# The low halves of the streamed weights: from GpSimd to VectorE in a two-layer hybrid encoder

## The chip, the core and the metric

The kernel runs on one core of a Trainium2 chip. The core has five engines that work side by side and meet at semaphores: TensorE (PE; its weight loads are listed as PEld), VectorE (DVE), ScalarE (ACT), GpSimd (POOL) and SyncE (SP), which here only issues transfers (DMA). Each engine works through its own queue in order: an instruction that waits holds up all that stand behind it. The metric is the time of one execution in device microseconds; several runs are told by their median.

## The reference

A trunk of two encoder layers over 1040 positions (16 learned ones ahead of 1024) with 1024 channels. Each layer has a mixer and a feed-forward part:

```
for l in range(DEPTH):
    h = h + hybrid_mixer(rmsnorm(h, norm1_w[l]), w_in[l], ...)
    h = h + swiglu(rmsnorm(h, norm2_w[l]), w_gate_up[l], w_down[l])
h = rmsnorm(h, final_norm_w)

def hybrid_mixer(h, w_in, conv_qkv_w, a_log, dt_bias, dn_norm_w, sc_conv_w, w_out):
    proj = h @ w_in
    qkv, z, b_raw, a_raw, sc_b, sc_c, sc_h = jnp.split(proj, idx, axis=-1)
    ...                      # q, k, v: short convolution, silu; q and k normalised
    o_fwd = chunk_gated_delta_rule(qp, kp, vp, gp[:, :, 0], bp[:, :, 0])
    o_bwd = flip(chunk_gated_delta_rule(flip(qp), flip(kp), flip(vp), ...))
    ...                      # o: sum of both, normalised, times silu(z)
    y_sc = sc_b * depthwise_conv_centred(sc_c * sc_h, sc_conv_w)
    return jnp.concatenate([o, y_sc], axis=-1) @ w_out

def swiglu(h, w_gate_up, w_down):
    gate, up = jnp.split(h @ w_gate_up, 2, axis=-1)
    return (jax.nn.silu(gate) * up) @ w_down
```

All of it is float32.

## The kernel before

**Products in two parts.** Channels lie on the 128 partitions, positions along the free axis. Each operand of a large product is split into a high part (the value rounded to a narrower float32 format that TensorE multiplies, `F32R`) and a low part (the rest). A product is then three matmuls: high weight by high x (line 157), high weight by low x (158), low weight by high x (159), all summed in one PSUM bank. `dense` (line 146) does this for a tile of 128 output channels, in two or three chunks of positions, and after each chunk takes the sum out of its bank (`evac`), on VectorE.

**How a weight tile is made.** `wload` (133) takes a tile in pieces of at most four 128x128 blocks, that is 128x512 elements. For each piece `wsplit` (124) issues the transfer of the raw weights on SP's queue (129), the high part on ScalarE (130) and the low part as raw minus high (131). Line 131 stands on VectorE where the flag `lov[0]` is set and on GpSimd elsewhere. Raw pieces have two buffers, high and low parts three each, so a high part waits until TensorE has left an earlier piece's buffer.

**Where line 131 runs.** `wload` and `wsplit` serve three products:

- the in-projection (`inproj`, 290), 28 tiles of two pieces in a layer. In the loop over `seq` (k heads, then q heads) the flag is set from the fifth tile on (line 632: `lov[0] = pos > 3`) and stays so through the v tiles; the loop behind them, with the gates z and the convolution group, sets it for its first two steps alone (line 738: `lov[0] = j < 2`). So of the 56 pieces of a layer 18 are on VectorE.
- the out-projection: eight pieces for the convolution half (918) and, in `out_part` (941), eight for each of two halves of the positions. The flag is not set.
- "the rest of down": four of the 22 blocks of the hidden axis, which the down projection takes as a plain product, eight pieces of four blocks. In layer 0 they are loaded between its chunks (1423, 1449), in layer 1 in one go by `last_weights` (1392). The flag is not set.

The gate-up projection and the larger part of down go by a seven-product scheme (Strassen's) with sums and differences of weight blocks and of x blocks; its weights are split by `w_op` (993, lines 997 and 998) and `w_unit`, whose low parts are on VectorE already.

**What else is on the two engines.** VectorE evacuates the banks (line 296 and 720 in the in-projection, 905 in the out-projection and rest of down), makes the low parts of x (178), does the short convolutions (309, 310), the triangular inversion (523, 525), the scan's state and outputs (795, 836, 858, 865, 868), and, in the second half of the out-projection, the scaled sums of x blocks for the seven-product scheme (`t_sum`, 977; `t_split`, 965) and the running sum of squares for the norm (950). GpSimd has, besides line 131, a few products with rstd (716, 732), with each other (729), a subtraction in `finalize` (857), most of the low parts of O (929) and some transfers (412, 415, 608 to 612).

**Order.** The program gives each instruction a priority (by its place in the text, or set by hand: `at_prio`, `mmp`, `evp`), and a planner (line 1573) simulates the engines and lays down each engine's queue from the priorities and from when it thinks that an instruction is ready. The delta-rule scan has high priority; the products of the in-projection fill TensorE between its steps. The out-projection follows: all eight tiles of the first half of the positions (`out_part(0, m)`), then all eight of the second (`out_part(1, m)`), with the sums of x blocks made beside the second.

Of the kernel before, what the change touches and what calls it, by code (L numbers as in the profile page):

```python
# [7 lines left out]
F32 = mybir.dt.float32  # L8
# [3 lines left out]
ALU = mybir.AluOpType  # L12
# [30 lines left out]
def trunk(ctx: ExitStack, tc: tile.TileContext, xT, w_in, w_ba, w_out, w_gu, w_dn,  # L43
# [8 lines left out]
    def nm(p):  # L52
        cnt[0] += 1
        return f"{p}_{cnt[0]}"
# [45 lines left out]
    tt = nc.vector.tensor_tensor  # L100
    stt = nc.vector.scalar_tensor_tensor
    ts = nc.vector.tensor_scalar
    ptt = nc.gpsimd.tensor_tensor
# [18 lines left out]
    lov = [False]  # L122

    def wsplit(src, hi, lo, raw=None):

        kk = src.shape[1]
        if raw is None:
            raw = wp.tile([128, WK, 128], F32, tag="raw", bufs=2, name=nm("raw"))
        dma(raw[:, 0:kk, :], src)
        whi_done[0] = act(out=hi, in_=raw[:, 0:kk, :], func=AF.Copy)  # L130
        (tt if lov[0] else ptt)(out=lo, in0=raw[:, 0:kk, :], in1=hi.bitcast(F32), op=ALU.subtract)  # L131

    def wload(src, nk):

        res = []
        step = min(nk, WK)
        for k0 in range(0, nk, step):
            kk = min(step, nk - k0)
            hi = wp.tile([128, WK, 128], F32R, tag="whi", name=nm("whi"))
            lo = wp.tile([128, WK, 128], F32R, tag="wlo", name=nm("wlo"))  # L140
            wsplit(src[:, k0:k0 + kk, :], hi[:, 0:kk, :], lo[:, 0:kk, :])
            for k in range(kk):
                res.append((hi[:, k, :], lo[:, k, :]))
        return res
# [135 lines left out]
    for l in range(DEPTH):  # L280
# [1111 lines left out]
        def last_weights(m):  # L1392
            if not fin_w:
                fin_w.append(flat(Y[0][2], F32R)[:, 0:4096].rearrange("p (m k e) -> p m k e", m=8, k=4))
                rows = [row(Y[1], F32R, 3) for _ in range(3)] + [row(Y[1] + "f", F32R)]
                fin_w.append([r[:, 512 * q:512 * q + 512].rearrange("p (k e) -> p k e", k=4) for r in rows for q in range(2)])
            hi, lo = fin_w[0][:, m], fin_w[1][m]
            wsplit(w_dn[l, m, :, 0:NF, :], hi, lo, raw4(("raw", "ck2")[m % 2]))
            wds.append([(hi[:, k], lo[:, k]) for k in range(4)])
# [11 lines left out]
        for u, (p, b, m) in enumerate(UNITS):  # L1411
# [16 lines left out]
            for j in range(NJ):  # L1428
# [9 lines left out]
                if b == NBK - 1:  # L1438
                    dh, z, op = TO[p]
# [138 lines left out]
```

## Time and profile before

| | |
|---|---|
| median of three runs | 2513.88 us |
| lowest, highest | 2511.24, 2517.37 us |
| the profiled execution, its own time | 2517.22 us |
| its span, first to last instruction | 2515.4 us |
| TensorE's granted clock, mean | 0.997 |
| matmuls | 17508 |
| transfers | 335.27 MB, mean 133 GB/s |

The profiler's page gives, for one execution, the busy time of each engine and its share of the span. A group of instructions is one line of the program on one engine: count, busy time, mean duration in ns, then the idle time of that engine just before them and what ended it. "Idle before <-ACT whi" means that the engine stood idle until ScalarE had finished the high part. In a list of instructions in order of time each row has its start, its duration, the engine, the line and the tiles (written <- read); in brackets stands the idle time before it. A table of windows gives the busy time of each engine within each stretch of the span. Matmuls overlap: the time from one start to the next is shorter than the duration shown, so counts of matmuls in equal windows say more of TensorE's pace than its busy share.

### The profile page before, as it was taken

The numbers are of one execution on the slowest core, as the hardware profiler recorded it, in microseconds if no ns is written. First come the engines' busy times: TensorE is split into PE (matmuls) and PEld (weight loads), VectorE is DVE, ScalarE is ACT, GpSimd is POOL, SyncE is SP. The second block draws the span as 40 slices with busy tenths as digits, with TensorE's granted clock in tenths as the row PEclk, the third lists the DMA queues.
The fourth block names the chain that finished last, engine by engine and source line by source line (L and its number), as shares of the span: only waits on it lengthen the run. The fifth ranks groups of instructions, "written<-read, shape, count | busy, mean of one in ns | idle before, by whom it ended". The sixth has DMA issues, their size and how long they took to land. (4 is left out here: it accounts for less than half of the span.)

```text
span 2515.4 us, 44862 instructions
## 1 busy us (share of the span) xinstructions
PE 2478.2 (99%) x17508; PEld 2276.9 (91%) x17508; DVE 1696.9 (67%) x3073; ACT 1045.9 (42%) x1944; POOL 340.0 (14%) x359
## 2 busy tenths in 40 slices
PE   8999999999999999999999999999999999999998
PEld 6989999999999999999999888998977888887887
DVE  4788333649877777877657893336698777677765
ACT  5554333535333333344445543335453333234444
POOL 1031212331000000000111212133400000000012
PEclk9999999999999999999999999999999999999999
DMA  3444353624323332764224443446332233238541
GB/s 127 135 166 149 112 161 130 212 77 136 116 102 102 108 102 81 256 198 133 92 77 145 152 154 116 143 131 205 120 126 101 97 105 117 90 112 279 177 120 68
DMA packets 199530, 335.27 MB, mean 133 GB/s; under 512 B 23404, under 2 KB 85668, under 8 KB 199316
## 3 DMA queue, kind: packets, MB, share of 16 engines
q1 hardware_dynamic: 171204, 293.84, 35.3%
q10 hardware_dynamic: 25936, 34.19, 4.2%
q0 software_dynamic: 2176, 4.36, 0.6%
q8 instruction: 138, 2.26, 0.4%
q14 instruction: 76, 0.62, 0.1%
HBM read 250.31 MB, written 81.99 MB: 132 GB/s over the span
## 5 line engine op out<-in xcount | busy, mean ns | idle before, releaser
L131 POOL TENSOR_TENSOR wlo<-raw,whi 128x512 fp32r<-128x512 f32 x132 | 176.4, 1338 | 1285.4 <-ACT whi L130 1116.7
L157 PE MATMUL pacc<-a,whi 128*128 128x346 f32 (+1 forms) x808 | 263.6, 329 | 8.8 <-ACT whi L130 7.6
L159 PE MATMUL pacc<-a,wlo 128*128 128x346 f32 (+1 forms) x808 | 262.4, 326 | 0.7 <-DVE wlo L131 0.5
L157 PE MATMUL pacc<-b,whi 128*128 128x346 f32 (+2 forms) x672 | 234.0, 349 | 2.4 <-ACT b L900 1.8
L159 PE MATMUL pacc<-b,wlo 128*128 128x346 f32 (+2 forms) x672 | 233.1, 348 | 0.8 <-DVE wlo L131 0.8
L158 PE MATMUL pacc<-a,whi 128*128 128x346 f32 (+1 forms) x688 | 225.1, 327 | 0.0
L130 ACT ACTIVATE whi<-raw 128x512 fp32r<-128x512 f32 x168 | 106.0, 631 | 228.3 <-PE pacc L158 124.9
L158 PE MATMUL pacc<-b,whi 128*128 128x346 f32 (+2 forms) x580 | 200.8, 346 | 0.0
L157 PEld LDWEIGHTS pacc<-a,whi 128*128 128x128 f32 x808 | 152.2, 189 | 14.6 <-ACT whi L130 8.1
L159 PEld LDWEIGHTS pacc<-a,wlo 128*128 128x128 f32 x808 | 152.9, 189 | 1.7 <-DVE wlo L131 0.8
L157 PEld LDWEIGHTS pacc<-b,whi 128*128 128x128 f32 x672 | 126.9, 189 | 14.5 <-issue 3.1
L159 PEld LDWEIGHTS pacc<-b,wlo 128*128 128x128 f32 x672 | 126.6, 189 | 9.8 <-DVE wlo L131 1.1
L158 PEld LDWEIGHTS pacc<-a,whi 128*128 128x128 f32 x688 | 130.3, 189 | 2.6 <-issue 2.1
L997 ACT ACTIVATE whi<-rw 128x512 fp32r<-128x512 f32 x92 | 57.6, 631 | 140.1 <-PE pf L1016 36.4
L158 PEld LDWEIGHTS pacc<-b,whi 128*128 128x128 f32 x580 | 109.5, 189 | 6.9 <-issue 0.4
L997 ACT ACTIVATE b<-rw 128x512 fp32r<-128x512 f32 x64 | 39.9, 631 | 135.0 <-PE pacc L1016 37.4
L296 DVE TENSOR_TENSOR a<-pacc,rstd 128x346 f32<-128x346 f32 (+2 forms) x59 | 32.7, 555 | 89.6 <-PE pacc L159 89.5
L296 DVE TENSOR_TENSOR b<-pacc,rstd 128x346 f32<-128x346 f32 (+1 forms) x63 | 32.5, 516 | 82.8 <-PE pacc L159 82.8
L131 POOL TENSOR_TENSOR a<-raw,a 128x512 fp32r<-128x512 f32 x3 | 3.9, 1285 | 597.1 <-ACT a L130 597.1
L997 ACT ACTIVATE a<-rw 128x512 fp32r<-128x512 f32 x64 | 40.0, 629 | 101.7 <-PE pacc L1016 60.3
L998 DVE TENSOR_TENSOR wlo<-rw,whi 128x512 fp32r<-128x512 f32 x92 | 62.8, 686 | 4.8 <-ACT whi L997 4.1
L1015 PE MATMUL pacc<-b,whi 128*128 128x260 f32 (+1 forms) x172 | 53.5, 311 | 0.7 <-ACT b L1051 0.7
(966 smaller groups left out, 8012.8 us busy)
## 6 DMA issues: line engine op xcount, KB each, us to landing
raw<-in_w_in SPq DMA_DIRECT2D x112, 256.0 KB, 2.5
raw<-in_w_gu SPq DMA_DIRECT2D x104, 256.0 KB, 2.9
rw<-in_w_gu SPq DMA_DIRECT2D x88, 256.0 KB, 3.0
rw<-in_w_dn SPq DMA_DIRECT2D x94, 192.0 KB, 2.7
rec<-vkd SPq DMA_DIRECT2D x61, 256.0 KB, 2.7
raw<-in_w_out SPq DMA_DIRECT2D x48, 256.0 KB, 2.8
b<-ad SPq DMA_DIRECT2D x45, 260.0 KB, 3.3
a<-ad SPq DMA_DIRECT2D x45, 256.0 KB, 5.2
```

The costliest lines, as they stand in the source:

```text
L130: whi_done[0] = act(out=hi, in_=raw[:, 0:kk, :], func=AF.Copy)
L131: (tt if lov[0] else ptt)(out=lo, in0=raw[:, 0:kk, :], in1=hi.bitcast(F32), op=ALU.subtract)
L157: mm(ps[:, :n], wh, xh[:, n0:n1], start=(k == 0), stop=False)
L158: mm(ps[:, :n], wh, xl[:, n0:n1], start=False, stop=False)
L159: mm(ps[:, :n], wl, xh[:, n0:n1], start=False, stop=(k == K - 1))
L296: tt(out=t[:, n0:n1], in0=ps, in1=rstd[:, n0:n1], op=ALU.mult)
L997: act(out=hi, in_=src, func=AF.Copy)
L998: tt(out=lo, in0=src, in1=hi.bitcast(F32), op=ALU.subtract)
L1015: mm(ps[:, :CW], w[0][:, k, :], th[:, cs], start=first and k == 0, stop=False, skip_group_check=True)
```

## The change

Line 131 no longer looks at the flag: each low part of `wsplit` is made on VectorE. The flag is still set at lines 632 and 738, and nothing reads it. Nothing else differs in the text of the program; the planner lays the queues anew.

```diff
@@ -128,7 +128,7 @@
             raw = wp.tile([128, WK, 128], F32, tag="raw", bufs=2, name=nm("raw"))
         dma(raw[:, 0:kk, :], src)
         whi_done[0] = act(out=hi, in_=raw[:, 0:kk, :], func=AF.Copy)
-        (tt if lov[0] else ptt)(out=lo, in0=raw[:, 0:kk, :], in1=hi.bitcast(F32), op=ALU.subtract)
+        tt(out=lo, in0=raw[:, 0:kk, :], in1=hi.bitcast(F32), op=ALU.subtract)
```

`tt` is VectorE's `tensor_tensor`, `ptt` GpSimd's.

## The prediction

> **What bounds the kernel now.** I read the page first, its busy line and its groups.
>
> ```profile
> span 2515.4 us, 44862 instructions
> PE 2478.2 (99%) x17508; PEld 2276.9 (91%) x17508; DVE 1696.9 (67%) x3073; ACT 1045.9 (42%) x1944; POOL 340.0 (14%) x359
> ```
>
> TensorE is busy for all but 37 us of the span. VectorE has a third of the span free, GpSimd nearly all of it. So work that changes engines counts only where TensorE ends up waiting for it. Next come the groups by line, different shapes apart, for the low parts on GpSimd and on VectorE (count, busy us, mean ns, idle us before them and who ended it), and TensorE's waits (us in total, times, longest).
>
> ```profile
> L131 POOL TENSOR_TENSOR wlo<-raw,whi 128x512 fp32r<-128x512 f32 x132 | 176.4, 1338 | 1285.4 <-ACT whi L130 1116.7 <-PE pacc L158 41.9 <-DMA raw<-in_w_in 38.8
> L131 DVE TENSOR_TENSOR wlo<-raw,whi 128x512 fp32r<-128x512 f32 x36 | 24.7, 686 | 1.9 <-ACT whi L130 1.6
> ```
>
> ```profile
> PE pacc L157 <- ACT whi L130: 8.7, 5, 5.9
> PE pacc L159 <- DVE wlo L131: 1.4, 2, 0.8
> ```
>
> GpSimd needs 1338 ns for a low part, VectorE 686. TensorE never waits for a low part from GpSimd: no such row stands in its waits. It waits twice, 1.4 us, for one of the 36 that VectorE makes already. The halves of a weight tile are made well ahead, so a faster subtraction alone gives nothing.
>
> Where could TensorE feel VectorE? I cut the run at the stages in which GpSimd makes low parts while VectorE is busiest: the two halves of the out-projection in both layers, the rest of down of layer 0, and the last weights (columns: us, then busy us and count of PE, PEld, DVE, ACT, POOL, clock, DMA share, GB/s; below them line 131 alone).
>
> ```profile
> 551.00:578.30 27.30, 27.30 (x231) 27.30 (x230) 18.25 (x36) 16.60 (x27) 11.71 (x10) 1.00 0.60 181
> 578.30:612.40 34.10, 31.88 (x262) 31.43 (x261) 33.99 (x53) 19.41 (x35) 6.20 (x4) 1.00 0.40 129
> 1795.00:1829.60 34.60, 34.60 (x294) 34.60 (x293) 27.99 (x50) 21.34 (x36) 15.31 (x12) 1.00 0.53 177
> 1829.60:1860.00 30.40, 27.60 (x155) 22.66 (x154) 30.36 (x46) 16.86 (x27) 3.57 (x2) 0.94 0.35 113
> 1231.00:1275.00 44.00, 44.00 (x277) 43.73 (x276) 36.44 (x66) 27.45 (x55) 11.97 (x8) 1.00 0.38 138
> 2436.00:2452.00 16.00, 16.00 (x71) 12.87 (x70) 6.00 (x9) 6.94 (x13) 11.70 (x13) 1.00 0.35 96
> ```
>
> ```profile
> 551.00:578.30 27.30, 0.00 (x0) 11.71 (x10) 1.00 0.60 181
> 2436.00:2452.00 16.00, 0.00 (x0) 10.54 (x8) 1.00 0.35 96
> ```
>
> In the second halves VectorE has no free time (33.99 of 34.10, 30.36 of 30.40) and TensorE loses 2.2 and 2.8 us. These two stages, where the next stage's operands are combined, decide most.
>
> **The change, part by part.** *What moves.* 132 subtractions of the first group and the 8 of the last weights (last row above): 140, the same operands, from GpSimd to VectorE. GpSimd loses 187 us (176.4 + 10.5), VectorE gains 140 x 0.686 = 96 us, 1697 to 1793 of 2515. No other instruction is added. The transfers of the raw weights on SP's queue stay; a raw buffer comes free some 0.6 us earlier (1338 - 686 ns), which is worth 0 as long as TensorE waits for no raw transfer, and no such row stands in its waits. On GpSimd's queue, what stood behind a low part (the subtractions and products of lines 716, 732, 857, 929, the transfers of 412 and 608) comes earlier; TensorE stands idle for none of it either. On VectorE's queue the moved instruction can stand before evacuations of matmul banks and before the x, T and scan operands: it waits for ScalarE's high part, and behind it TensorE may wait for a bank or an operand. Where it stands is chosen by the planner, which orders every engine anew.
>
> *Cost in the queue (1).* The 36 on VectorE delayed TensorE by 1.4 us: 0.039 us each, times 140 is 5.4 us. Lower end 0: most of the 140 meet an emptier VectorE than those 36. Upper end: twice it, 10.8, if the waits of the banks behind them add as much. I take 5.4, since it is the only row that shows low parts on this queue.
>
> *The out-projection (2).* In the first halves VectorE is free for 9.1 and 6.6 us and gets 10 and 12 low parts. One costs a full queue 0.60 us, from start to start:
>
> ```profile
> 586.88 0.68 DVE L998 TENSOR_TENSOR wlo<-raw,whi 128x512 fp32r<-128x512 f32 x1
> 587.48 0.42 DVE L905 TENSOR_TENSOR a<-pf,a 128x260 f32<-128x260 f32 x1
> ```
>
> That is 6.0 and 7.2 us: hidden in the first, 0.6 us over in the second, if nothing else gets shorter. Without that cover all 13.2 us would push the full halves. In the full halves there are 4 and 2 low parts: 2.4 and 1.2 us, 3.6 in all, with nothing to hide under. Against that stands what GpSimd does to VectorE there:
>
> ```profile
> 578.60 1.79 DVE L977 SCALAR_TENSOR_TENSOR a<-a,npar 128x520 f32<-128x520 f32 x1
> 583.37 0.68 DVE L950 TENSOR_TENSOR rstd<-rstd,sq 128x520 f32<-128x520 f32 x1
> 586.21 0.74 DVE L977 SCALAR_TENSOR_TENSOR a<-a,npar 128x520 f32<-128x520 f32 x1
> 587.82 1.65 DVE L950 TENSOR_TENSOR rstd<-rstd,sq 128x520 f32<-128x520 f32 x1
> 595.92 1.78 DVE L977 SCALAR_TENSOR_TENSOR a<-a,par,a 128x520 f32<-128x520 f32 x1
> 1832.74 1.66 DVE L950 TENSOR_TENSOR rstd<-rstd,sq 128x512 f32<-128x512 f32 x1
> 1840.69 1.79 DVE L977 SCALAR_TENSOR_TENSOR b<-b,par,b 128x512 f32<-128x512 f32 x1
> ```
>
> ```profile
> 578.54 1.29 POOL L131 TENSOR_TENSOR wlo<-raw,whi 128x512 fp32r<-128x512 f32 x1 [1.39 <-ACT whi L130]
> 587.62 1.30 POOL L131 TENSOR_TENSOR wlo<-raw,whi 128x512 fp32r<-128x512 f32 x1 [4.73 <-DVE wlo L998]
> 595.01 2.13 POOL L131 TENSOR_TENSOR wlo<-raw,whi 128x512 fp32r<-128x512 f32 x1 [6.10 <-PE pf L158]
> 1832.55 1.29 POOL L131 TENSOR_TENSOR wlo<-raw,whi 128x512 fp32r<-128x512 f32 x1 [5.40 <-DVE wlo L998]
> 1839.66 2.28 POOL L131 TENSOR_TENSOR wlo<-raw,whi 128x512 fp32r<-128x512 f32 x1 [5.81 <-ACT whi L130]
> ```
>
> The same line takes 0.74 us (586.21) or 1.79 (578.60), and 0.68 or 1.65. Each long one reads two tensors from SBUF and overlaps a GpSimd subtraction; it ends as that one does. The five cost 1.05, 0.97, 1.04, 0.98 and 1.05 us, 5.1 together, against 3.6 for the same low parts on VectorE. So the ends are -1.5 us (all of the stretch goes and TensorE follows one for one) and +4.2 (3.6 and the 0.6, no relief). I take +0.7, below the middle, because the stretched rows are on the engine that bounds the stage, but its gain is capped by TensorE's waits there.
>
> *Rest of down (3).* VectorE has 7.6 us free of 44.0 and gets 8 x 0.60 = 4.8: hidden, 0. Its cover is thin: TensorE loses nothing there now, and without the cover it would be up to 4.8 us. The last weights: 10.0 of 16.0 us are free, 4.8 needed: 0.
>
> *Clock (4).* Around the end of the scan and in the second full half of layer 1 the clock drops when TensorE has stood still.
>
> ```profile
> 1730.00:1735.00 5.00, 3.20 (x22) 2.65 (x20) 4.03 (x5) 1.92 (x6) 3.79 (x3) 1.00 1.02 381
> 1735.00:1740.00 5.00, 4.75 (x17) 3.88 (x17) 5.00 (x10) 5.00 (x14) 0.00 (x0) 0.66 1.01 407
> 1845.00:1850.00 5.00, 3.56 (x21) 2.78 (x19) 5.00 (x10) 3.21 (x6) 0.00 (x0) 1.00 0.40 131
> 1850.00:1855.00 5.00, 4.12 (x10) 3.00 (x11) 5.00 (x8) 4.27 (x7) 0.00 (x0) 0.66 0.39 131
> 1855.00:1860.00 5.00, 5.00 (x28) 3.49 (x27) 4.96 (x8) 2.08 (x4) 0.00 (x0) 1.00 0.19 63
> ```
>
> The window at clock 0.66 passes 10 matmuls instead of 28: 18/28 of 5 us is 3.2 us lost, 0.9 of it idle, so 2.3 us is the clock. A new wait of this size pays it once more, a removed one gets it back: between -4.6 (both drops go) and +4.6 (two more). I take +0.5, since a fuller queue adds waits more readily than a re-ordered one removes them.
>
> *Sum.* 5.4 + 0.7 + 0 + 0.5 = +6.6 us. The profiled execution took 2517.2 us by its own time, 1.8 us of it outside the span, and becomes 2523.8. The median of the runs shown is 3.3 us lower; against it the forecast is 2513.9 + 6.6 = **2520.5 us**, slower by 0.26%.
>
> **The rivals.** *A, VectorE becomes the bound of the out-projection: slower by more.* A low part on VectorE waits at the head of its queue for ScalarE's high part, which waits for TensorE to leave its buffer: the rows at 595.01 and 1839.66 stood 6.10 and 5.81 us before they could start. If VectorE stands still for a third of that, 2 us, at each of the six low parts in the full halves, that is 12 us, plus two clock drops, 4.6: 2513.9 + 16.6 = 2530. It decides once VectorE's free time there goes below the waits, and there is none. Against it: the planner can put other work first, and the 36 on VectorE idle 1.9 us in all.
>
> *B, the stretch goes and the time falls.* If the full halves lose their 5.1 us of stretch for 3.6 us of work, and the chain that ends the scan (line 1290 at 1.74 us and line 865 at 1.22, elsewhere 0.69 and 0.17, rows below) loses its 2.1, the waits of TensorE there can shrink: 2.2 and 2.8 us in the full halves, 1.8 + 0.3 at 1730 to 1740, and two drops of 2.3. All of it is 11.7; 60%, since not every wait in these windows hangs on a stretched row, is 7: 2507.
>
> ```profile
> 1730.94 1.74 DVE L1290 TENSOR_TENSOR rw<-rw,rw 128x512 f32<-128x512 f32 x1 [3.33 <-POOL a3f L857]
> 1732.60 1.22 DVE L865 SCALAR_TENSOR_TENSOR st<-st,g 128x4 f32<-128x4 f32 x1
> 1741.34 0.17 DVE L865 SCALAR_TENSOR_TENSOR st<-st,g 128x4 f32<-128x4 f32 x1
> 636.74 0.69 DVE L1290 TENSOR_TENSOR rw<-rw,rw 128x512 f32<-128x512 f32 x1 [0.69 <-DMA rw<-in_w_gu]
> ```
>
> The Trainium skill speaks for B: "GPSIMD Engine Reference", section Specifications, says that GpSimd's SBUF interfaces are shared with VectorE, with contention for VectorE instructions that have two SBUF inputs. The trace agrees: 0.74 against 1.79 us for one line. Against B: TensorE waits at few places, and the moved work lands on the same full queue.
>
> *C, hidden either way.* The 96 us fall into VectorE's 818 free ones, the queue cost is near 0, gains and losses of the full halves cancel: 2514, give or take 5.
>
> **How the numbers follow.** Two runs of this kernel can differ by about 0.2%, 5 us; that is my bound of no change. The forecast holds 0.30 (2519 to 2526), A 0.20, B 0.30, C 0.20. Slower is forecast and A, 0.50; faster is B, 0.30; the same is C, 0.20. The likeliest sign is slower, so the time given is the forecast's, whose own range is 2514 (queue cost 0, the rest as summed) to 2528 (5.4 more in the queue and the clock once more). The range for 8 in 10 reaches down into B, to 2504 (10 us of the 11.7), and up through A to 2538 (a second third of the stand-still at two to four of the six).
>
> **What would show it.** Right: rows of TensorE waiting for low parts of line 131 on VectorE, about four times the 1.4 us; the full halves as long as before or longer; VectorE busy somewhat under 1793 us, by as much stretch as goes. Line 977 and line 950 at 0.74 and 0.68 us throughout would show that the stretch was GpSimd's. For A: idle time of VectorE ended by ScalarE's high part between the first and the second half of the out-projection. For B: no clock below 1.00 at the end of the scan and after the out-projection, and fewer than 2 us lost in each full half. Wrong altogether: a time beyond 2538 or under 2504, which would mean that the planner's new order moved the matmuls themselves, far from line 131.

## The result, and the profile after

| | before | changed |
|---|---|---|
| median of 14 runs each | 2516.23 us | 2509.51 us |
| lowest, highest | 2511.24, 2518.01 us | 2506.66, 2514.66 us |
| ratio, 95% interval | | 0.9975 (0.9968 to 0.9982) |
| the profiled execution, its own time | 2517.22 us | 2510.77 us |

The changed kernel is 6.7 us faster by the medians; by the ratio 0.25% (0.18 to 0.32%), 6.3 us. Forecast was 6.6 us slower: the sign was wrong. Rival B had been priced at 7 us faster.

The page of the changed kernel, its span and the busy time of the engines:

```profile
span 2507.8 us, 44856 instructions
PE 2476.0 (99%) x17508; PEld 2277.4 (91%) x17508; DVE 1753.8 (70%) x3213; ACT 1050.2 (42%) x1946; POOL 160.3 (6%) x219
```

VectorE has exactly 140 instructions more (3073 to 3213). At 686 ns they would be 96.0 us, but its busy time, which counts overlapping instructions once, rose by only 56.9. Added up row by row, the durations of all VectorE instructions outside line 131 fell from 1837.77 to 1803.33 us: 34.4 us went out of them, without their number changing. Two lines that the prediction named show it: one line's instructions in min/median/max ns, with the first and last start, first in the kernel before:

```profile
L977 DVE SCALAR_TENSOR_TENSOR a<-a,npar x4: 744/1102/1794, 578.6 to 591.1; 128x520 f32<-128x520 f32 x4
L950 DVE TENSOR_TENSOR rstd<-rstd,sq x28: 676/692/1657, 556.1 to 1855.0; 128x520 f32<-128x520 f32 x14, 128x512 f32<-128x512 f32 x14
```

and in the changed one:

```profile
L977 DVE SCALAR_TENSOR_TENSOR a<-a,npar x4: 750/752/754, 581.5 to 594.8; 128x520 f32<-128x520 f32 x4
L950 DVE TENSOR_TENSOR rstd<-rstd,sq x28: 678/691/705, 558.9 to 1851.5; 128x520 f32<-128x520 f32 x14, 128x512 f32<-128x512 f32 x14
```

The minimum stayed and the maximum fell to it: 1794 to 754 ns, 1657 to 705. The moved group itself, and TensorE's longest waits (us in total, times, longest), in the changed kernel:

```profile
L131 DVE TENSOR_TENSOR wlo<-raw,whi 128x512 fp32r<-128x512 f32 x168 | 122.0, 726 | 77.7 <-ACT whi L130 70.4
```

```profile
PE pacc L157 <- ACT whi L130: 6.7, 3, 5.6
PE pa L424 <- ACT kt L426: 3.9, 4, 2.9
...
PE pacc L159 <- DVE wlo L131: 1.0, 2, 0.8
```

VectorE now stands 70.4 us at the head of its queue for ScalarE's high part. TensorE's wait for these low parts did not grow with their number: 1.4 us for 36 of them before, 1.0 us for 168 now. The windows of the changed kernel, the first four moved along to the same stages as the prediction's, the others at the same times (us, busy us and count of PE, PEld, DVE, ACT, POOL, clock, DMA share, GB/s):

```profile
553.80:581.10 27.30, 27.30 (x230) 27.30 (x229) 22.91 (x44) 16.64 (x27) 0.00 (x0) 1.00 0.58 184
581.10:613.20 32.10, 30.96 (x258) 30.75 (x257) 32.10 (x57) 20.40 (x36) 0.00 (x0) 1.00 0.42 134
1792.20:1826.90 34.70, 34.70 (x295) 34.70 (x294) 31.30 (x62) 21.59 (x36) 0.00 (x0) 1.00 0.53 174
1826.90:1853.50 26.60, 26.00 (x158) 21.62 (x158) 26.60 (x45) 17.02 (x26) 0.00 (x0) 1.00 0.38 129
1231.00:1275.00 44.00, 44.00 (x278) 43.92 (x276) 36.73 (x74) 27.21 (x54) 0.00 (x0) 1.00 0.39 136
1730.00:1735.00 5.00, 3.96 (x27) 3.26 (x25) 3.80 (x9) 3.44 (x11) 1.34 (x1) 1.00 1.01 368
1735.00:1740.00 5.00, 4.60 (x21) 3.79 (x22) 5.00 (x9) 4.91 (x17) 0.00 (x0) 1.00 1.02 410
```

In the full halves (second and fourth row) VectorE still has no free time, but it comes through them sooner: about the same matmuls now take 32.1 us instead of 34.1, and 26.6 instead of 30.4. TensorE stands 1.1 and 0.6 us in them, where it stood 2.2 and 2.8. The clock is 1.00 in these windows; the two at 0.66 are gone. Two other drops have come instead, in layer 0, in windows at 1.00 in the profile before:

```profile
100.00:105.00 5.00, 3.23 (x14) 2.69 (x13) 5.00 (x12) 1.89 (x3) 0.22 (x1) 0.80 0.98 338
145.00:150.00 5.00, 3.16 (x15) 3.17 (x16) 2.51 (x4) 2.95 (x5) 0.00 (x0) 0.73 0.61 177
```

TensorE's mean granted clock is 0.997 in both profiles, so the clock as a whole gave nothing in this pair.

Where in the run the time came off is read from landmarks that both traces have: line 905 (evacuations of the out-projection and of the rest of down) and, in layer 1, the last of the early sums of line 1051. Same view as above, before:

```profile
L905 DVE TENSOR_TENSOR a<-pacc,a x58: 415/511/521, 497.5 to 1272.5; 128x346 f32<-128x346 f32 x25, 128x260 f32<-128x260 f32 x20, 128x348 f32<-128x348 f32 x13
L905 DVE TENSOR_TENSOR b<-pacc,b x50: 408/424/694, 1742.9 to 2505.8; 128x256 f32<-128x256 f32 x29, 128x512 f32<-128x512 f32 x21
L905 DVE TENSOR_TENSOR b<-pf,b x22: 408/416/691, 1796.6 to 2502.7; 128x256 f32<-128x256 f32 x19, 128x512 f32<-128x512 f32 x3
L1051 ACT ACTIVATE a3f<-pacc x1: 598/598/598, 1870.4 to 1870.4; 128x512 f32<-128x512 f32 x1
```

and changed:

```profile
L905 DVE TENSOR_TENSOR a<-pacc,a x58: 420/513/522, 500.4 to 1272.7; 128x346 f32<-128x346 f32 x25, 128x260 f32<-128x260 f32 x20, 128x348 f32<-128x348 f32 x13
L905 DVE TENSOR_TENSOR b<-pacc,b x50: 410/426/693, 1741.5 to 2498.2; 128x256 f32<-128x256 f32 x29, 128x512 f32<-128x512 f32 x21
L905 DVE TENSOR_TENSOR b<-pf,b x22: 410/424/691, 1794.6 to 2495.0; 128x256 f32<-128x256 f32 x19, 128x512 f32<-128x512 f32 x3
L1051 ACT ACTIVATE a3f<-pacc x1: 598/598/598, 1864.5 to 1864.5; 128x512 f32<-128x512 f32 x1
```

Changed minus before: +2.9 us at the start of layer 0's out-projection (500.4 against 497.5), +0.2 at the end of layer 0's rest of down, -1.4 at the start of layer 1's out-projection, -2.0 at the start of its last product, that of `out_part` (line 905 reading `pf`), -5.9 behind it, -7.6 at the end. So in this pair of profiles layer 0 ends where it did, and half of layer 1's gain (3.9 us) lies in that last product, by the windows in its full half (30.4 to 26.6 us). A second profile of the changed kernel (the changed kernel again, below) has +0.7, -1.6, -3.0, -3.6, -6.4 and -8.5 at the same places: one such difference is good to some 2 us.

### The profile page after: what moved, and what is told of

It reads as the page before. It is cut to its first block, busy times and chain, and to the rows that moved or that the text cites. A ratio compares the mean times of both kernels' runs of the same rounds, so it can differ in the third digit from the quotient of the medians.

```text
span 2507.8 us, 44856 instructions
## 1 busy us (share of the span) xinstructions
PE 2476.0 (99%) x17508; PEld 2277.4 (91%) x17508; DVE 1753.8 (70%) x3213; ACT 1050.2 (42%) x1946; POOL 160.3 (6%) x219
## 5 line engine op out<-in xcount | busy, mean ns | idle before, releaser
L131 DVE TENSOR_TENSOR wlo<-raw,whi 128x512 fp32r<-128x512 f32 x168 | 122.0, 726 | 77.7 <-ACT whi L130 70.4
```

The lines of the kernel that those rows point to most:

```text
L131: tt(out=lo, in0=raw[:, 0:kk, :], in1=hi.bitcast(F32), op=ALU.subtract)
```

## The experiments

Each is compared with runs of the kernel before that were taken beside it; its median there was 2516.28 us for the first four, 2516.87 for the next three, 2519.01 for the last three. A ratio is against that.

| experiment | median, us | ratio (95% interval) |
|---|---|---|
| `out_part`'s 32 low parts alone moved | 2512.53 | 0.9980 (0.9971 to 0.9988) |
| all but those 32 moved | 2516.40 | 1.0003 (0.9994 to 1.0011) |
| changed, with idle subtractions on GpSimd | 2517.57 | 1.0002 (0.9994 to 1.0011) |
| changed, with idle memsets on GpSimd | 2511.66 | 0.9983 (0.9974 to 0.9991) |
| layer 1 alone moved | 2511.63 | 0.9978 (0.9969 to 0.9987) |
| changed, out-projection's low parts made twice | 2521.19 | 1.0015 (1.0006 to 1.0025) |
| changed, scan-end work moved too | 2506.48 | 0.9964 (0.9952 to 0.9976) |
| the changed kernel again | 2510.11 | 0.9965 (0.9952 to 0.9978) |
| scan-end and in-projection work moved too | 2510.15 | 0.9961 (0.9946 to 0.9975) |
| scan-end work and the last scaling moved too | 2510.03 | 0.9964 (0.9950 to 0.9978) |

**One part alone.** The kernel before, with only the 32 low parts of the out-projection's last product on VectorE:

```diff
-        (tt if lov[0] else ptt)(out=lo, ...
+        (tt if lov[0] or gp[0] else ptt)(out=lo, ...
...
-            dense(wload(w_out[l, m, :, 0:4, :], 4), os_, hcut[z], add_h(m), pwide)
+            gp[0] = True; dense(wload(w_out[l, m, :, 0:4, :], 4), os_, hcut[z], add_h(m), pwide); gp[0] = False
```

> The kernel before, with the 32 low parts of out_part (both halves, both layers) on VectorE and the other 108 still on GpSimd. Theory (the gain is the end of GpSimd's stretching of VectorE's two-input instructions where VectorE is full): between the two profiles the out-projection of layer 0 gained 2.4 us and that of layer 1 3.7 us, so this alone is 6 us faster than before (2510), and lines 977 and 950 stand at 0.75 and 0.69 us in the full halves. Rival 1 (the planner's new order of all queues made the gain): little or nothing is left, within 3 us of before, either sign. Rival 2 (GpSimd's other work, freed from low parts in its queue, comes sooner): GpSimd's work beside the scan is as before, so nothing is gained.

By the ratio it gained 5.0 us (3.0 to 7.3). The second clock drop stayed in its profile, that of the slowest of its eleven runs (windows):

```profile
1845.00:1850.00 5.00, 3.02 (x12) 1.98 (x11) 5.00 (x8) 3.20 (x6) 0.00 (x0) 0.93 0.40 119
1850.00:1855.00 5.00, 5.00 (x18) 3.99 (x17) 4.88 (x8) 2.17 (x4) 0.00 (x0) 0.73 0.26 83
```

So most of the gain is the out-projection's. Whether its faster runs had that drop too, one profile cannot tell.

**All the others.** The changed kernel, with those 32 back on GpSimd and the other 108 (in-projection, convolution half of the out-projection, rest of down) on VectorE:

```diff
-        tt(out=lo, ...
+        (ptt if gp[0] else tt)(out=lo, ...
```

> The changed kernel, with the 32 low parts of out_part back on GpSimd. Theory: what is left is the end of the scan of layer 1 (3.0 us gained between the profiles) and the loss in layer 0 ahead of the out-projection (2.8 us): within 2 us of before (2514 to 2518). Rival 1: a new order again, any value. Rival 2: the work of GpSimd beside the scan still comes sooner, so at least half of the gain stays, 3 us or more faster than before.

+0.8 us (-1.5 to +2.8): three quarters of the moved work, its gains and costs taken together, changed nothing that can be told. The stretch is back where the 32 are; the row of line 950 in this kernel:

```profile
L950 DVE TENSOR_TENSOR rstd<-rstd,sq x28: 678/695/1653, 558.2 to 1859.0; 128x520 f32<-128x520 f32 x14, 128x512 f32<-128x512 f32 x14
```

**GpSimd busy again, queues as they are.** The gain could have come from GpSimd's work beside VectorE, or from the planner's new order. So in the changed kernel GpSimd got work whose result nobody reads, at the same places: behind each high part of those 32 pieces two subtractions of 128x256 elements of a tile of its own, or five memsets of it. (As in the diff of the 32 alone, `gp[0]` is set around `out_part`'s product only; it holds the tile here. The same goes for the doubled low parts below.) The queues of TensorE, VectorE and ScalarE are entry by entry those of the changed kernel.

```diff
-        tt(out=lo, ...)
+        tt(out=lo, ...); [after(ptt(out=gp[0], in0=gp[0], in1=gp[0], op=ALU.subtract), whi_done[0]) for _ in range(2) if gp[0] is not None]
```

> The changed kernel, and behind each high part of out_part two GpSimd subtractions of 128x256 on a spare tile that nothing reads: GpSimd is as busy as before (1.4 us a piece), while the queues of TensorE, VectorE and ScalarE stay in the changed kernel's order, entry by entry. Theory: rows of 977 and 950 stretch to 1.4 to 1.8 us again, and the 6 us of the out-projection are lost: 2514 to 2517. Rivals 1 and 2: the order and GpSimd's own useful work are the changed kernel's, so the time stays at 2509 to 2511.

```diff
-        tt(out=lo, ...)
+        tt(out=lo, ...); [after(nc.gpsimd.memset(gp[0], 0.0), whi_done[0]) for _ in range(5) if gp[0] is not None]
```

> As the run with two dummy subtractions, but with five GpSimd memsets of 128x256 on the spare tile, which read nothing, for about the same 1.3 us a piece. If VectorE is held by what GpSimd reads, it stays at the changed kernel's time (2509 to 2511) and lines 977 and 950 stay at 0.75 and 0.69 us; if any GpSimd instruction holds VectorE, it goes to 2514 to 2517 as with the subtractions. Rivals 1 and 2: 2509 to 2511 as well, so this run tells only what of GpSimd holds VectorE.

With subtractions the whole gain went (1.0002), with memsets most of it stayed (0.9983). GpSimd's added time was about the same, as the groups show, first with subtractions, then with memsets:

```profile
L131 POOL TENSOR_TENSOR spare<-spare 128x256 f32<-128x256 f32 x64 | 52.4, 819 | 89.5 <-ACT whi L130 86.9
```

```profile
L131 POOL MEMSET spare<- 128x256 f32 x160 | 50.2, 314 | 88.1 <-ACT whi L130 80.7
```

VectorE's own rows tell them apart; for the same 3213 instructions it is busy 1763.8 us with subtractions, 1752.4 with memsets and 1753.8 in the changed kernel. With subtractions:

```profile
L977 DVE SCALAR_TENSOR_TENSOR b<-b,npar x4: 737/814/1104, 1824.9 to 1839.2; 128x512 f32<-128x512 f32 x4
L950 DVE TENSOR_TENSOR rstd<-rstd,sq x28: 675/763/1110, 559.1 to 1858.0; 128x520 f32<-128x520 f32 x14, 128x512 f32<-128x512 f32 x14
L1051 ACT ACTIVATE a3f<-pacc x1: 598/598/598, 1872.7 to 1872.7; 128x512 f32<-128x512 f32 x1
```

With memsets:

```profile
L977 DVE SCALAR_TENSOR_TENSOR b<-b,npar x4: 742/744/745, 1822.7 to 1836.4; 128x512 f32<-128x512 f32 x4
L950 DVE TENSOR_TENSOR rstd<-rstd,sq x28: 681/688/700, 560.0 to 1854.5; 128x520 f32<-128x520 f32 x14, 128x512 f32<-128x512 f32 x14
L1051 ACT ACTIVATE a3f<-pacc x1: 598/598/598, 1867.7 to 1867.7; 128x512 f32<-128x512 f32 x1
```

The subtractions stretch line 950 to 1110 ns, the memsets leave it at 700, and the landmark behind layer 1's out-projection comes at 1872.7 against 1867.7 us. The expected 1.4 to 1.8 us were not reached: each subtraction of a pair is shorter than the one before the change. The place of one stretch, from the list in order of time of the kernel with subtractions (GpSimd's row is the first of a pair):

```profile
1834.47 1.10 DVE L977 SCALAR_TENSOR_TENSOR b<-b,npar 128x512 f32<-128x512 f32 x1
...
1834.21 0.82 POOL L131 TENSOR_TENSOR spare<-spare 128x256 f32<-128x256 f32 x1 [5.39 <-ACT whi L130]
```

VectorE's row ends 0.54 us after that subtraction (1834.21 + 0.82 is 1835.03; 1834.47 + 1.10 is 1835.57). With the order held, GpSimd's two-input subtractions alone undo the gain: the rival that the new order by itself made it falls. Memsets read nothing, and they kept most of it, so what decides is not that GpSimd is busy. The Trainium skill, "SBUF — State Buffer", section "Who interferes with whom", has this rule: a VectorE instruction with two SBUF inputs contends with a GpSimd instruction that reads SBUF, not with one that only writes it. Both runs agree, 1110 against 700 ns at most for line 950.

**Layer 1 alone.** Layer 0 had lost 2.9 us ahead of its out-projection. Does leaving layer 0 as it was give more?

```diff
-        tt(out=lo, ...
+        (tt if lov[0] or gp[0] else ptt)(out=lo, ...
...
-        last = l == DEPTH - 1
+        last = gp[0] = l == DEPTH - 1
```

> The kernel before, with all low parts of layer 1 on VectorE; layer 0 has them where it had them. Theory: between the profiles of before and changed, layer 0 ends with nothing gained (2.8 us lost ahead of its out-projection, 2.4 gained in it) and layer 1 gains 7.7 us, so this gains all of it: 2508 to 2510, 6 to 8 us faster than before, level with the changed kernel. Rival (layer 0's gain in the out-projection is carried to the end): half of the gain, 2513.

It gained 5.5 us (3.3 to 7.8), which lies between the two expectations and whose interval holds the changed kernel's ratio. Layer 1 carries most of the gain; that layer 0's loss is worth avoiding is not shown. (Layer 0's out-projection starts at 495.7 us here and at 497.5 in the profile before, with its low parts on the same engines.)

**The cost of one low part, by doubling it.** The changed kernel, with each of the 32 subtractions of the out-projection done twice (the second writes the same values again):

```diff
-        tt(out=lo, ...)
+        [tt(out=lo, ...) for _ in range(2 if gp[0] else 1)]
```

> The changed kernel, with each of the 32 low parts of out_part made twice on VectorE (the same subtraction again). This doubles the suspected cost in the queue of VectorE, without GpSimd. Theory: a low part costs its 0.60 us where VectorE is full: six of them in the full halves are 3.6 us; the first halves have 4.4 and 3.4 us free for 6.0 and 7.2 us of it, so 1.6 and 3.8 us more are pushed on: 9.0 us slower than the changed kernel if TensorE follows one for one, 2518; half of that, 2514, if its waits take up half. Rival (VectorE's queue is no bound there): 2510.

Against the changed kernel it lost 0.40% (1.0015 less 0.9975), 10 us, some 7 to 13 by the two intervals, near the 9.0 expected from VectorE's queue setting TensorE's pace there one for one. The planner laid the queues anew for it, so part of this may be a new order. The windows show that the full half of layer 0 has grown and that TensorE stands in it:

```profile
553.80:581.10 27.30, 26.82 (x225) 26.61 (x223) 25.31 (x49) 14.27 (x24) 0.00 (x0) 1.00 0.46 146
581.10:620.00 38.90, 35.27 (x277) 33.79 (x278) 37.68 (x65) 21.54 (x37) 0.00 (x0) 1.00 0.45 137
```

TensorE is busy 35.27 of 38.90 us, 3.6 us lost, with 277 matmuls; in the changed kernel it lost 1.1 us in 32.10 with 258.

**Further along the same way.** If GpSimd's two-input work costs VectorE time, what is left of it could move as well: the subtractions that end the scan (857, 929), those and three products of the in-projection (716, 729, 732), or those and the last scaling (1465).

```diff
-                ptt(out=o, in0=o, in1=qs[0:n], op=ALU.subtract)
+                tt(out=o, in0=o, in1=qs[0:n], op=ALU.subtract)
...
-                (tt if n0 == o0 else ptt)(out=ol[:, h, n0:n1], ...
+                tt(out=ol[:, h, n0:n1], ...
```

> The changed kernel, with the other two-input GpSimd work beside the scan's end on VectorE too: line 857 (16 subtractions) and line 929 (24 low parts of O). In the changed kernel's profile these still stretch VectorE (line 868 to 2.40 us, line 865 to 1.02 us). Theory: the same exchange as for the low parts: the stretch goes, VectorE has free time there, TensorE's waits of 1.4 us in the two windows from 1730 to 1740 us shrink: 1 to 2 us faster than the changed kernel (2508). Rival: 40 more instructions in VectorE's queue at the end of the scan, which the out-projection waits for, cost more than the stretch: 2 us or more slower (2512).

The next kernel is the changed one unaltered, as a measure for the two behind it.

> The changed kernel once more, for the two runs beside it: 2509 to 2511, 0.25% faster than before.

```diff
-            ptt(out=t0, in0=t0, in1=rstd, op=ALU.mult)
+            tt(out=t0, in0=t0, in1=rstd, op=ALU.mult)
...
-                ptt(out=t2[:, o0:L], in0=t2[:, o0:L], in1=t1[:, o0:L], op=ALU.mult)
+                tt(out=t2[:, o0:L], in0=t2[:, o0:L], in1=t1[:, o0:L], op=ALU.mult)
...
-                ptt(out=t2, in0=t2, in1=rstd, op=ALU.mult)
+                tt(out=t2, in0=t2, in1=rstd, op=ALU.mult)
```

> The run with lines 857 and 929 on VectorE, and the six products of lines 716, 729 and 732 of each layer as well (16 of about 1.24 us, some 20 us of VectorE, in stages where it has a third to two thirds of its time free). Theory: their stretch (line 716 alone held a 0.22 us instruction to 1.3 us and more in the profile of before) goes too, but the stages beside the scan keep TensorE busy anyhow: level with the run with 857 and 929, 2506, give or take 2. Rival (each GpSimd instruction with two inputs costs TensorE something): 2 us or more below it.

```diff
-                    pend = [lambda q=q, n0=n0, n1=n1, mul=tt if n0 == 16 and q > 5 else ptt: scaled(...
+                    pend = [lambda q=q, n0=n0, n1=n1, mul=tt: scaled(...
...
-                mul, by = (ptt, sv) if q in (3, 6) else (tt, pb)
+                mul, by = tt, pb
```

> The run with lines 857 and 929 on VectorE, and the 16 products of the last norm (line 1465) that were on GpSimd. In the profile of the changed kernel GpSimd's products there stretch line 189, the running sum of squares (0.42 us) to as much as 1.2 us, ahead of the last matmuls. Theory: at the very end nothing hides it, so 1 to 2 us are gained: 2505. Rival (VectorE then has the products themselves in its queue ahead of the sums): 2 us slower, 2508.

0.9964, 0.9961 and 0.9964 stand beside 0.9965 for the changed kernel: inconclusive among themselves. All lie 0.35 to 0.39% under the kernel before, and none is shown to be better than the changed one. The second of the three took away stretch that the first had left: line 868's longest row is 2405 ns in the changed kernel, still 2202 in the first, beside a GpSimd product of line 732, and 693 in the second. The time did not follow, so stretch there costs nothing that can be told.

## Why the prediction was wrong, point by point

The sum was +6.6 us, the result -6.3 by the ratio. Two terms carry most of the difference: the cost in the queue (+5.4 forecast, +0.8 measured) and the out-projection (+0.7 forecast, -5.0 measured). The measured two come to -4.2; the rest is within their intervals.

**The bound (held).** TensorE stayed the bound at 99%, and the second halves of the out-projection were the places where VectorE decides. Doubling the low parts there cost the end about what the queue's overflow was reckoned at.

**Cost in the queue, +5.4 us (the step that failed first).** It divided the 1.4 us of waits among 36 low parts and multiplied by 140. TensorE's waits for line 131 are 1.0 us with 168, and the 108 pieces outside `out_part`, for which this step would give 4.2 us, cost 0.8 net (at most 2.8). The waits belonged to two moments, not to each piece. Where the moved work did make TensorE wait was in layer 0's in-projection, at other rows than those multiplied: this one, which the profile before does not have, and those at line 424 (3.5 us between 60 and 160 us, against 1.5).

```profile
PE pacc L157 <- DVE b L296: 1.6, 1, 1.6
```

That is an evacuation behind the low parts, the kind of wait that the term's upper end allowed for. "Most of the 140 meet an emptier VectorE" stood there as a reason for the lower end, 0; the value should have been taken from it. The low end of the forecast's own range, 2514 with no queue cost, does not follow from the sum either: 2513.9 + 0.7 + 0.5 is 2515.1.

**The out-projection, +0.7 us (ends -1.5 and +4.2; wrong in sign and outside its ends).** Alone it gave -5.0 us (-7.3 to -3.0). The price of the moved work was sound: the doubled low parts cost 10 us where 9.0 were expected. The gain was sized too small. It counted five long rows of the full halves, 5.1 us. Before the change there was a sixth there, and others in the first halves, of which two are shown:

```profile
582.00 1.45 DVE L977 SCALAR_TENSOR_TENSOR a<-a,npar 128x520 f32<-128x520 f32 x1
1823.12 1.54 DVE L977 SCALAR_TENSOR_TENSOR b<-b,npar 128x512 f32<-128x512 f32 x1
1826.25 1.45 DVE L977 SCALAR_TENSOR_TENSOR b<-b,npar 128x512 f32<-128x512 f32 x1
```

By the whole of their rows lines 977 and 950 lost 8.9 us (29.2 to 24.2 and 23.3 to 19.3). Of the 32 rows of line 977 before, the six that overlap a GpSimd subtraction took 1448 to 1794 ns, the other 26 took 736 to 761. The full halves became 2.0 and 3.8 us shorter, with their six low parts still in them; 1.1 and 2.2 us of that are waits of TensorE that went, and in layer 1 the drop went too. The rows were also misread in a detail: "it ends as that one does". They end 0.54 to 0.56 us after GpSimd's instruction (578.60 + 1.79 against 578.54 + 1.29). That fits a row that stands until GpSimd is through and then does most of its own work. The price of 1 us for each of the five was right all the same.

**Rest of down and last weights, 0 (held).** In 1231 to 1275 TensorE is busy 44.00 of 44.00, with 278 matmuls against 277; in the 16 us of the last weights it is busy throughout, now as before.

**Clock, +0.5 us (0 in the profiles; price too high).** The two drops named went, but two others came at 103 and 147 us, so the low end of -4.6 was not reached, though the named stages look like it. A drop was also priced too high. The 2.3 us came from comparing 10 matmuls with 28, of which eight have half as many columns; a window of 5 us at 0.66 lacks 0.34 x 5 = 1.7 us. The reason given, that a fuller queue adds waits, fits the two new drops, each of which follows one of the waits of TensorE in layer 0's in-projection.

**The rivals.** B held in mechanism for the out-projection; that its price came so near, 7 us against 6.7, is partly luck. Of its 11.7 us of TensorE's losses, the full halves gave back 1.1 and 2.2 and the scan end's waits 0.7 (1.0 and 0.4 us left, of 1.8 and 0.3), 4.0 together; the two drops, 4.6 in its sum, were worth some 3.4 and were replaced by two others. With the 32 of the out-projection left on GpSimd, moving the rest gained nothing. Its chance of 0.30 was too small: the stretched rows had been seen and their cause named. Of the signs listed, VectorE's busy time under 1793 us came (1753.8); four times the wait for low parts and longer full halves did not. A fell: VectorE stood 70.4 us for high parts, but not in the full halves, where it was busy 32.10 of 32.10 and 26.60 of 26.60 us. C fell too, since the full halves became shorter.

**What stays open.** How much the moved work costs layer 0 ahead of its out-projection. The waits at lines 296 and 424 stand in all nine profiles with layer 0's in-projection low parts moved, and in the three without them line 296 has none and line 424 0.8 to 1.6 us. But the out-projection starts at 494.8 to 501.5 us in the nine and at 495.7 to 497.5 in the three, so the loss is not separated from the spread. Nor is it settled what gave the last 1.7 us between 1864.5 us and the end, nor how much of the gain needs the planner's new order besides the end of the stretch.

## What to carry to other kernels

An instruction moved off an engine that shares memory access with the bottleneck's feeder may cost less than its duration says: look at the minimum and the maximum of the same line and shape, and whether the long rows overlap the neighbour's; if they do, the difference is time that the neighbour takes. Count them all, in the stages ahead too. A wait seen a few times is not to be multiplied by the number of instructions; find the stage where the queue is full and price that stage. Count clock drops over the whole run, since some go and others come. To tell contention from a new order, put the neighbour's load back as idle work into the changed kernel, and vary what it reads.

## What the hardware showed beside that

With GpSimd's 140 subtractions 34.4 us went from VectorE's other instructions, 0.25 us for each on average, where the same subtraction costs VectorE's queue 0.60 us; only in the full stages, where a row is held for about 1 us, does leaving it on GpSimd cost more. The holding goes both ways: two of GpSimd's rows in the prediction, 2.13 and 2.28 us against 1.29 elsewhere, began while a two-input VectorE row of 1.23 us (line 965, from 594.76 and 1839.56) was under way, and the next row of line 977 was held behind them in turn. VectorE's evacuations of line 905, with one input in PSUM and one in SBUF, were not held: before, 59 of the 152 overlap arithmetic on GpSimd, and they take no longer than the others of their shape (408 to 426 ns for 128x256 in both).

The clock fell after some short stalls and not after others of the same length. In the kernel with only the 32 moved the only wait of TensorE between 1843 and 1852 us is this one (us, times, longest):

```profile
PE pb L1015 <- ACT whi L997: 2.0, 1, 2.0
```

The next 5 us ran at 0.73. With the idle subtractions it was 1.9 us, and two windows ran at 0.87 and 0.79. With the idle memsets it was 1.9 us as well, and the clock stayed at 1.00:

```profile
1845.00:1850.00 5.00, 3.00 (x14) 2.03 (x13) 5.00 (x10) 3.85 (x6) 0.00 (x0) 1.00 0.48 154
1850.00:1855.00 5.00, 5.00 (x22) 3.95 (x23) 5.00 (x7) 3.60 (x6) 0.00 (x0) 1.00 0.25 79
```

With the scan-end and in-projection work moved, where nothing is stretched, it was 1.9 us again, and 1845 to 1850 ran at 0.66. So neither the stretch nor the length of the stall settles by itself whether a drop follows; these runs do not show what does.
